# Seven-product passes that run on from chunk to chunk, and a last chunk that joins them, in a two-layer encoder

## The chip, the cores and the metric

The kernel runs on one core of a Trainium2 chip. Its engines are TensorE (PE, matrix products into PSUM; its weight loads are PEld), VectorE (DVE), ScalarE (ACT), GpSimd (POOL) and SyncE (SP, which issues most DMAs). The metric is the device time of one execution in microseconds. Each engine runs its instructions in the order in which they are written down for it; semaphores order the engines among each other.

## The reference

Two layers on an input of 256 tokens by 2048 channels, all in float32. Layer 0 mixes the tokens by pooling and attention, layer 1 by a chunkwise matrix memory; after each comes a gated MLP:

```python
def conv_ffn(x, w_up, conv_w, conv_b, w_down):
    u = x @ w_up
    up = jnp.pad(u, ((0, 0), (1, 1), (0, 0)))
    c = conv_w.astype(u.dtype)
    u = c[0] * up[:, :-2] + c[1] * up[:, 1:-1] + c[2] * up[:, 2:] + conv_b.astype(u.dtype)
    gate, val = jnp.split(u, 2, axis=-1)
    return (jax.nn.silu(gate) * val) @ w_down
...
        x = x + mixed
        x = x + conv_ffn(rms_norm(x, norm_ffn[layer]), w_up[layer], conv_w[layer], conv_b[layer], w_down[layer])
```

`w_up` is 2048 x 11264, `w_down` 5632 x 2048. The change touches only the product with `w_down`.

## The kernel before

Each float32 matrix is split into a high and a low float32r part, and a product is three matmuls: high by high, high by low, low by high. A weight block of 128 x 1024 numbers (512 KB) comes by a DMA from SP's queue into `w` (six buffers), ScalarE writes the high part into `hl` and VectorE the low part (four buffers); that is the split of a block. Everything that needs weights takes them from one stream, in the order in which PE uses them. The instructions of PE stand as the program writes them; VectorE's, ScalarE's and SP's are placed by a scheduler.

The MLP walks over 44 blocks of 128 hidden channels, in chunks of 4, 8, 8, 8, 8 and 8 blocks (chunks 0 to 5). `up` makes one block: 64 matmuls from four weight blocks (11.14 us of PE), then ScalarE and VectorE make the convolution and the gate and leave the block in `g`, high and low.

The product with `w_down` of chunk c runs in the gaps between the `up`s of chunk c + 1. Two blocks of `g` are a pair; the output has two halves of 1024 columns (half 0 and half 1), each of two blocks of 512. A direct product (`dn`) of a pair with a half is a 2 by 2 block product of eight products. The kernel instead uses the seven-product scheme of Strassen and Winograd: an A pass makes four products per pair (12 matmuls) and a B pass three (9 matmuls), with sums of `g` blocks (made by `combine`, in the plan called `mix`: four VectorE instructions and two high-low splits) and sums of weight blocks. Each product has its own PSUM bank (`pp`, four banks in the pool `ps`, A uses all four, B three), which accumulates over the pairs of one chunk. At the end of a pass `drain` adds the banks into `acc` or `x`: four instructions after A, three after B, by ScalarE the first time for some and else by VectorE. After a half's last pass `total` adds `acc` into `x` in eight VectorE instructions. Chunk 1 of layer 0 uses the scheme for half 1 only and goes direct for half 0; chunk 5 of both layers goes direct in all four blocks: `down_two` for blocks 0 and 1, `down` for blocks 2 and 3 (in layer 1 block 3 is `down_end`, the `end` matmuls). In layer 1 each block of `x` then goes to `out` by SP's queue.

The weight sums of an A pass come in two ways. For half 0 a task (`premix`) makes them long before in DRAM with DMAs (`m`), and the stream loads the result. For half 1 the stream makes them as it goes: a `Sum` is one DMA on SP's queue and a second, adding one on POOL's queue into a `sum` buffer (three buffers); a `Chain` is a load to which VectorE adds the sum (`w<-w,sum`, then `w<-w`) before it is split. So an A pass of half 1 loads three blocks per pair and costs VectorE two adds more; an A pass of half 0 loads two; a B pass one and a half.

`_ffn_plan` writes the order. Behind each `up` stands a slot with one unit: two pairs of a pass (one pair in chunk 1 of layer 0). The pass order was A, B of half 1 and then A, B of half 0, in each chunk anew. Below, A1 is an A pass of half 1, an A1 step an `up` with a unit of A1 behind it, and so on. `pp` and a chunk number in a name stand for a product of that chunk; `_14` is half 1, product 4.

Of the kernel before, what the change touches and what calls it, by code (L numbers as in the profile page):

```python
# [16 lines left out]
P = 128  # L17
# [17 lines left out]
BOTH = ((0, 2, 3, 4), (0, 1, 2, 3, 4))  # L35
NEG = -1.0e30
# [173 lines left out]
def trunk(ctx: ExitStack, tc: tile.TileContext, gx, xT, xn, call, catt, cml, weights, mixes, out):  # L210
# [749 lines left out]
    def ffn_layer(layer, norm, nxt):  # L960
        with ExitStack() as es:
# [7 lines left out]
            combos, pss, quads, seen = {}, {}, {}, set()  # L969
# [86 lines left out]
            def drain(kind, c, h, order):  # L1056
# [15 lines left out]
                if kind == "B" and c == len(FCH) - 2:  # L1072
                    wv.add(total(h), 1.5)
# [59 lines left out]
            def down_two(c):  # L1133

                gt, n = gts[c], FCH[c]
                pss2 = [mmp.tile([P, 2, 512], F32, tag="mm", name=f"dn{layer}_{c}_{b}") for b in range(2)]
                for kts in (range(n - 2), range(n - 2, n)):
                    for ps in pss2:
                        mov_part(ps, lambda k: gt[:, k], list(kts), kts[0] == 0, kts[-1] == n - 1)
                wv.until(lambda: ("A", 0) not in seen or ("total", 0) in pss)  # L1140
                for b, ps in enumerate(pss2):
# [8 lines left out]
            for kind, c, i, *j in _ffn_plan(layer):  # L1150
# [9 lines left out]
                elif kind == "two":  # L1160
                    down_two(c)
# [65 lines left out]
def _halves(layer, c):  # L1227

    return () if c in (-1, len(FCH) - 1) else (0, 1) if c in BOTH[layer] else (1,)


def _ffn_plan(layer):

    seq = []
    for c, n in enumerate(FCH):
        pairs = FCH[c - 1] // 2 if c else 0  # L1240
        halves = _halves(layer, c - 1)

        if halves == (0, 1):
            slots = [[(kind, c - 1, h, js)] for h in (1, 0) for kind in "AB"
                     for js in ((0, 1), (2, 3))[: pairs // 2]]
            slots = [[]] * (pairs < 4) + slots
        else:
            slots = [[(kind, c - 1, 1, (j,))] for kind in "AB" for j in range(pairs)]
            for b in range(2 if pairs else 0):
                slots[(b + 1) * pairs // 2 - 1].append(("down", c - 1, b))  # L1250

        busy = {j: k for k, slot in enumerate(slots) for u in slot if u[0] == "A" for j in u[3]}
        for i in range(n):
            seq.append(("up", c, i))
            seq += slots[i] if i < len(slots) else []
            if c < len(FCH) - 1:
                seq += [("mix", c, j) for j in range(n // 2) if i == max(2 * j + 1, busy.get(j, 0))]
    return seq + [("two", len(FCH) - 1, 0)] + [("down", len(FCH) - 1, b) for b in range(2, NB)]


def _down_chunks(layer, w):
# [3 lines left out]
    for c, n in enumerate(FCH):  # L1265
        rows = w[k0 * P : (k0 + n) * P]
        blocks = [_mov(rows[:, b * 512 : b * 512 + 512]) for b in range(NB) if b // 2 not in _halves(layer, c)]
# [5 lines left out]
    n = sum(FCH[:-1]) // 2  # L1273
# [12 lines left out]
def _ffn_weights(layer, up, parts):  # L1286
# [3 lines left out]
    for kind, c, i, *j in _ffn_plan(layer):  # L1290
# [3 lines left out]
        elif kind in ("down", "two"):  # L1294
            out += [next(down) for _ in range(FCH[c] // 2 * (2 if kind == "two" else 1))]
# [119 lines left out]
```

## Time and profile before

| | |
|---|---|
| time, median of 3 runs | 2163.43 us (2162.89 to 2163.73) |
| profiled execution | 2163.78 us, its span 2162.0 us |
| PE, weight loads, VectorE, ScalarE, POOL busy | 2156.2, 1844.2, 1734.7, 1414.3, 212.7 us |
| MLP of layer 0 | from 257 to 972 us of the span, the seven-product passes from 325 to 925 |
| MLP of layer 1 | from 1450 to the end, the passes from 1518 to 2115 |
| all `pp` matmuls | 1428, 361.8 us busy |
| all `dn` and `end` matmuls | 480, 111.3 us busy |
| DMA | 555.29 MB, mean 257 GB/s |

Busy time is the time in which at least one instruction of an engine ran. Instructions of PE overlap, so the mean duration of a matmul is longer than the distance between two. In the chain of waits a row is a start, a duration and a piece of work, and the chain is followed back from the last instruction; where it stays on PE, PE never waited.

### The profile page before, as it was taken

To read this page: it belongs to the slowest core of one execution; us is meant where nothing else is said; L and a number is where in the kernel's file an instruction comes from. 1 tells how busy PE (TensorE), PEld (TensorE's weight loads), DVE (VectorE), ACT (ScalarE), POOL (GpSimd) and SP (SyncE) were. 2 spreads that over 40 slices of the span, in tenths; PEclk is the share of its full clock that TensorE was granted. 3 is DMA by queue.
4 is the path that set the end of the run, shared out by engine and by line. 5 is a ranking of instruction groups with operands and counts; after the bars stand their busy time and mean duration, and the time that the engine had idled before them with its cause. 6 is when DMAs were issued, how large, how long until landed. Compare 5 with 4: busy or idle time off the path is not lost.

```text
span 2162.0 us, 31902 instructions
## 1 busy us (share of the span) xinstructions
PE 2156.2 (100%) x11412; PEld 1844.2 (85%) x11412; DVE 1734.7 (80%) x2425; ACT 1414.3 (65%) x2208; POOL 212.7 (10%) x268
## 2 busy tenths in 40 slices
PE   9999999999999999999999999999999999999999
PEld 7888888888888888889888888888888888888887
DVE  7686688887988988986777676667889898988896
ACT  7665578766777767666454544457777777776763
POOL 0022111110100100001111111211100000000000
PEclk9999999999999999999999999999999999999999
DMA  9668989898999877779888888898978787887774
GB/s 323 213 202 250 287 250 311 248 280 247 298 296 293 287 257 232 266 232 252 231 246 251 237 250 230 273 276 249 289 226 285 258 283 246 265 262 251 233 249 162
DMA packets 164097, 555.29 MB, mean 257 GB/s; under 512 B 20602, under 2 KB 23202, under 8 KB 163938
## 3 DMA queue, kind: packets, MB, share of 16 engines
q1 hardware_dynamic: 129632, 462.88, 62.0%
q0 software_dynamic: 20704, 52.71, 14.8%
q10 hardware_dynamic: 13602, 37.67, 5.7%
q8 instruction: 89, 1.46, 0.3%
q14 instruction: 70, 0.57, 0.1%
HBM read 551.04 MB, written 69.25 MB: 287 GB/s over the span
## 4 chain that ended last, share of the span: by engine, by line
PE 97%; DVE 2%; DMA 1%; issue 0%; ACT 0%; DVEq 0%
PE up L264 44%; PE pp L264 15%; PE op L264 8%; PE dn L264 5%; PE mv L264 4%; PE mq L264 4%; PE mk L264 4%; PE mo L264 4%; PE qproj L264 3%; PE kproj L264 1%; PE vproj L264 1%; PE pool L264 1%; DVE hl L128 1%; PE qk L264 1%; PE av L264 1%; PE end L264 1%
## 5 line engine op out<-in xcount | busy, mean ns | idle before, releaser
L128 DVE TENSOR_TENSOR hl<-w,hl 128x1024 fp32r<-128x1024 f32 (+2 forms) x840 | 1009.4, 1214 | 218.4 <-ACT hl L127 216.0
L127 ACT CAST hl<-w 128x1024 fp32r<-128x1024 f32 (+2 forms) x839 | 863.4, 1047 | 451.4 <-PE up L264 145.3
L264 PE MATMUL up<-xx,hl 128*128 128x512 f32 (+1 forms) x5632 | 994.0, 337 | 0.0
L264 PEld LDWEIGHTS up<-xx,hl 128*128 128x128 f32 x5632 | 866.9, 188 | 130.9 <-DVE hl L128 0.5
L264 PE MATMUL pp<-hl,s 128*128 128x512 f32 x816 | 204.9, 392 | 0.3 <-DVE hl L128 0.3
L264 PEld LDWEIGHTS pp<-hl,s 128*128 128x128 f32 x816 | 150.4, 188 | 32.0 <-DVE hl L128 1.2
L473 POOL DMA_DIRECT2D m<-m x128 | 102.1, 800 | 701.0 <-PE up L264 293.1
L264 PE MATMUL pp<-hl,g 128*128 128x512 f32 x612 | 156.9, 391 | 0.0
L427 ACT COPY tb_up<-up 128x512 f32<-128x512 f32 x88 | 51.6, 587 | 123.4 <-PE up L264 123.2
L264 PEld LDWEIGHTS pp<-hl,g 128*128 128x128 f32 x612 | 112.2, 188 | 22.3
L991 ACT ACTIVATE y<-tb_up,conv 128x256 f32<-128x256 f32 x176 | 104.4, 593 | 0.0
L992 DVE TENSOR_TENSOR y<-y,z 128x510 f32<-128x510 f32 x88 | 60.7, 689 | 52.2 <-ACT y L991 52.2
L473 POOL DMA_DIRECT2D m<-in_dn x64 | 54.6, 853 | 468.1 <-PE dn L264 168.1
L264 PE MATMUL dn<-hl,g 128*128 128x512 f32 x432 | 100.3, 391 | 0.0
L428 DVE TENSOR_TENSOR tb_up<-up,tb_up 128x512 f32<-128x512 f32 x88 | 60.8, 691 | 49.2 <-ACT tb_up L427 48.9
L264 PEld LDWEIGHTS dn<-hl,g 128*128 128x128 f32 x432 | 80.6, 188 | 16.6
L989 ACT ACTIVATE z<-tb_up,conv 128x256 f32<-128x256 f32 x176 | 88.9, 505 | 5.1 <-DVE tb_up L984 4.2
L264 PE MATMUL mk<-xx,hl 128*128 128x512 f32 (+1 forms) x512 | 92.2, 337 | 0.0
L264 PE MATMUL mq<-xx,hl 128*128 128x512 f32 (+1 forms) x512 | 92.1, 337 | 0.0
L264 PE MATMUL mv<-hl,xx 128*128 128x512 f32 (+2 forms) x480 | 91.7, 350 | 0.0
L264 PE MATMUL op<-hl,cat 128*128 128x512 f32 x384 | 91.6, 393 | 0.0
L264 PE MATMUL mo<-hl,xx 128*128 128x512 f32 x384 | 90.5, 391 | 0.0
(232 smaller groups left out, 2196.5 us busy)
## 6 DMA issues: line engine op xcount, KB each, us to landing
w<-in_up SPq DMA_DIRECT2D x352, 512.0 KB, 4.8
w<-in_dn SPq DMA_DIRECT2D x176, 512.0 KB, 4.6
w<-in_m_in SPq DMA_DIRECT2D x124, 512.0 KB, 5.1
m<-in_dn ACTq DMA_DIRECT2D x128, 256.0 KB, 5.5
w<-m SPq DMA_DIRECT2D x64, 512.0 KB, 5.0
w<-in_a_in SPq DMA_DIRECT2D x46, 512.0 KB, 5.3
sum<-in_dn SPq DMA_DIRECT2D x36, 512.0 KB, 5.4
sum<-in_dn POOLq DMA_DIRECT2D x36, 512.0 KB, 9.1
```

The source lines that it names most:

```text
L127: (self.nc.vector.tensor_copy if i + c == 0 else self.nc.scalar.copy)(hl[:, 0, c : c + n], w[:, c : c + n])
L128: low = self.nc.vector.tensor_sub(hl[:, 1, c : c + n], w[:, c : c + n], hl[:, 0, c : c + n].bitcast(F32))
L264: last_mm[0] = pe.matmul(out_, lhsT, rhs, start=start, stop=stop, skip_group_check=True)
L427: a.copy(tb, ps[:, :, 1, :])
L428: v.tensor_add(tb, ps[:, :, 0, :], tb)
L473: paced(eng.dma_start(to[p : p + P // 2], src[p : p + P // 2], **kw))
L989: a.activation(z[:, 0, j, :], u[:, j, :], AF.Copy, scale=cw(tl, 0))
L991: a.activation(y[:, j, :], u[:, j, :], AF.Identity, scale=cw(tl, 1), bias=cw(tl, 3))
L992: v.tensor_add(y[:, :, 1:S], y[:, :, 1:S], z[:, 0, :, 0 : S - 1])
```

## The change

Passes are now listed by hand, per layer and chunk. Where the last pass of a chunk and the first of the next are of the same kind and half, they are one pass: its banks are not drained between the chunks and the first product of the second does not start the bank anew. `first`, `last` and `end` of a unit are worked out from its neighbours. Layer 0 has four such joints (A1 from chunk 0 to 1, B1 from 1 to 2, B0 from 2 to 3, B1 from 3 to 4), layer 1 three (B1 from 0 to 1, B0 from 1 to 2, B1 from 2 to 3). 38 passes become 31.

In layer 1 the first two pairs of chunk 5 leave the direct path for half 1. Their A products join the A1 pass of chunk 4 and their B products its B1 pass; blocks 2 and 3 go direct with the other two pairs alone. For that, the order in chunk 5 of layer 1 is A0, A1, A1 of the new pairs, B0, B1, B1 of the new pairs. The last B1 unit of chunk 4 has no `up` behind it, and the unit of the new pairs stands between the first 36 direct matmuls of block 0 and the rest of `down_two`. total(1) follows at the very end, total(0) one `up` before the end. Two combinations more are made in chunk 5.

```diff
+LAST = (0, 4)
+PASSES = (
+    ("B0 A0 B1 A1", "A1 B1", "B1 A1 A0 B0", "B0 A1 A0 B1", "B1 A1 A0 B0"),
+    ("B0 A1 A0 B1", "B1 A1 A0 B0", "B0 A1 A0 B1", "B1 A1 A0 B0", "A0 A1 A1+ B0 B1 B1+"),
+)
...
-            def unit(kind, c, h, js):
-                n = FCH[c] // 2
+            def unit(kind, c, h, js, first, last, end):
...
-                if js[0] == 0:
+                if first:
...
-                    product(pss[e], x_, wh, wl, j == 0, j == n - 1)
-                if js[-1] == n - 1:
+                    product(pss[e], x_, wh, wl, first and j == js[0], last and j == js[-1])
+                if last:
                     pss["busy"] = True
-                    wv.add(drain(kind, c, h, order), 0.6)
+                    wv.add(drain(kind, h, order, end), 0.6)
...
-                if kind == "B" and c == len(FCH) - 2:
+                if end:
                     wv.add(total(h), 1.5)
...
-                kts = list(range(FCH[c]))
+                kts = list(range(_direct(layer, c, b), FCH[c]))
...
+            def down_two(c, second):
...
+                parts = [(ps, kts) for kts in (range(n - 2), range(n - 2, n)) for ps in twos]
+                for ps, kts in parts[1:] if second else parts[:1]:
+                    mov_part(ps, lambda k: gt[:, k], list(kts), kts[0] == 0, kts[-1] == n - 1)
+                if not second:
+                    return
...
+def _pairs(layer, c):
+    return (LAST[layer] if c == len(FCH) - 1 else FCH[c]) // 2
+def _direct(layer, c, b):
+    return LAST[layer] if c == len(FCH) - 1 and b >= NB // 2 else 0
...
+    for c in range(len(FCH) - 1):
+        at = max(at + (c == 0) * FCH[0], sum(FCH[: c + 1]))
+        step = len(_halves(layer, c))
+        for pas in PASSES[layer][c].split():
+            k = c + pas.endswith("+")
+            for j in range(0, _pairs(layer, k), step):
+                units.append((pas[0], k, int(pas[1]), tuple(range(j, j + step))))
+                to = slots[min(at, FT - 1)] if at <= FT else late
+                to.append(len(units) - 1)
...
+                at += 1
+    for n, u in enumerate(units):
+        first, last = (not 0 <= m < len(units) or (units[m][0], units[m][2]) != (u[0], u[2]) for m in (n - 1, n + 1))
+        units[n] = u[:4] + (first, last, all(o[2] != u[2] for o in units[n + 1 :]))
...
+    seq += [("two", c, 0)] + [units[e] for e in late] + [("two", c, 1)]
+    return seq + [("down", c, b) for b in range(2, NB)]
```

Three places show what moves. The first is VectorE in layer 0, at the last `up` of chunk 2 (`y_19` is its block): before, the B1 pass of chunk 1 is drained here (`pp_1_10` to `pp_1_12`), between the splits and the sum adds (`w<-w,sum`) of the A1 pass of chunk 2.

```order
L128 TENSOR_TENSOR hl_5252<-w_5174,hl_5252 128x1024
L123 TENSOR_TENSOR w_5270<-w_5270,sum_5150 128x512
L128 TENSOR_TENSOR hl_5272<-w_5199,hl_5272 128x1024
L1068 TENSOR_TENSOR acc_2469<-acc_2469,pp_1_10_4847 128x512
L1068 TENSOR_TENSOR x<-x,pp_1_11_4848 128x512
L128 TENSOR_TENSOR hl_5294<-w_5240,hl_5294 128x1024
L1068 TENSOR_TENSOR x<-x,pp_1_12_4849 128x512
L123 TENSOR_TENSOR w_5314<-w_5314,sum_5196 128x512
L124 TENSOR_TENSOR w_5270<-w_5270 128x512
L992 TENSOR_TENSOR y_19_5226<-y_19_5226,z_19_5227 128x2x255
```

Now the B1 pass of chunk 2 follows with no drain and no sum adds at this place:

```order
L134 TENSOR_TENSOR hl_5240<-w_5163,hl_5240 128x1024
L134 TENSOR_TENSOR hl_5260<-w_5185,hl_5260 128x1024
L134 TENSOR_TENSOR hl_5282<-w_5226,hl_5282 128x1024
L998 TENSOR_TENSOR y_19_5212<-y_19_5212,z_19_5213 128x2x255
L999 TENSOR_TENSOR y_19_5212<-y_19_5212,z_19_5213 128x2x255
L134 TENSOR_TENSOR hl_5303<-w_5238,hl_5303 128x1024
```

The three drain adds and the sum adds have left this place; they stand two `up`s later, together.

The second is SP in layer 1, in the second half of chunk 5: before, the loads here were premixed sums of half 0 (`m_14`, `m_15`) between those of two `up`s.

```order
L107 DMA w_19367<-in_up 128x1024
L107 DMA w_19378<-m_14_13061 128x1024
L107 DMA w_19390<-m_14_13061 128x1024
L107 DMA w_19413<-m_15_13327 128x1024
L107 DMA w_19435<-m_15_13327 128x1024
L107 DMA w_19456<-in_up 128x1024
```

Now the sums of the second and third A1 step stand there (the first three of the run are issued long before):

```order
L118 DMA sum_19183<-in_dn 128x1024
L113 DMA w_19230<-in_dn 128x1024
L118 DMA sum_19291<-in_dn 128x1024
L113 DMA w_19270<-in_dn 128x1024
L113 DMA w_19294<-in_up 128x1024
L113 DMA w_19345<-in_up 128x1024
L113 DMA w_19359<-in_up 128x1024
L113 DMA w_19372<-in_up 128x1024
L118 DMA sum_19356<-in_dn 128x1024
L113 DMA w_19393<-in_dn 128x1024
```

Four loads of finished sums became three sums in the ring of three buffers, and the loads to which they are added.

The third is PE at the end of layer 1, behind the last `up`. Before, the last B0 products of chunk 4 are followed by direct products alone (block 0, block 1, then the last pair of each):

```order
L264 MATMUL pp_4_02_19809<-hl_19948,s_4_3_18793 128x512 x3
L264 MATMUL dn_5_0_19979<-hl_19959,g_5_18798 128x512 x12
L264 MATMUL dn_5_0_19979<-hl_19970,g_5_18798 128x512 x12
L264 MATMUL dn_5_0_19979<-hl_19983,g_5_18798 128x512 x12
L264 MATMUL dn_5_1_19980<-hl_20001,g_5_18798 128x512 x12
```

Now the B1 pass stays open over the first 36 matmuls of block 0 and takes the new pairs of chunk 5 in (`g_5`, `s_5`):

```order
L270 MATMUL pp_4_12_19932<-hl_19971,s_4_3_18745 128x512 x3
L270 MATMUL dn_5_0_20005<-hl_19983,g_5_18750 128x512 x12
L270 MATMUL dn_5_0_20005<-hl_19995,g_5_18750 128x512 x12
L270 MATMUL dn_5_0_20005<-hl_20009,g_5_18750 128x512 x12
L270 MATMUL pp_4_10_19930<-hl_20026,g_5_18750 128x512 x3
L270 MATMUL pp_4_11_19931<-hl_20026,g_5_18750 128x512 x3
L270 MATMUL pp_4_10_19930<-hl_20043,g_5_18750 128x512 x3
L270 MATMUL pp_4_11_19931<-hl_20043,g_5_18750 128x512 x3
L270 MATMUL pp_4_12_19932<-hl_20060,s_5_0_19224 128x512 x3
L270 MATMUL pp_4_12_19932<-hl_20060,s_5_1_19340 128x512 x3
L270 MATMUL dn_5_1_20006<-hl_20071,g_5_18750 128x512 x12
```

Eighteen matmuls of the B1 pass came in; blocks 2 and 3 have two rows of twelve instead of four each. Over the whole program PE has 24 matmuls of A and 18 of B more and 48 direct ones fewer; VectorE 22 drain adds fewer; SP three loads and POOL two adding DMAs more.

More of the change, by code (lines that the diff above doesn't have):

```diff
@@ L1227, in _halves @@
 def _halves(layer, c):
[L1229 to L1252 removed]
+    return () if c == len(FCH) - 1 else (0, 1) if c in BOTH[layer] else (1,)
@@ L1253, in _ffn_plan @@
         for i in range(n):
             seq.append(("up", c, i))
[L1255 to L1258, printed above, removed]
+            mixes = [(busy.get((c - 1, j), 0) - f0, ("mix", c, j)) for j in range(_pairs(layer, c))]
+            mixes = [(k, e) for k, e in mixes if i == max(2 * e[2] + 1, k)]
@@ L1266, in _down_chunks @@
         rows = w[k0 * P : (k0 + n) * P]
-        blocks = [_mov(rows[:, b * 512 : b * 512 + 512]) for b in range(NB) if b // 2 not in _halves(layer, c)]
+        blocks = [_mov(rows[_direct(layer, c, b) * P :, b * 512 : b * 512 + 512]) for b in range(NB) if b // 2 not in _halves(layer, c)]
         if c == len(FCH) - 1:
@@ L1294, in _ffn_weights @@
         elif kind in ("down", "two"):
-            out += [next(down) for _ in range(FCH[c] // 2 * (2 if kind == "two" else 1))]
+            n = FCH[c] // 2 - 1
+            out += [next(down) for _ in range((n, n + 2)[i] if kind == "two" else (FCH[c] - _direct(layer, c, i)) // 2)]
         elif kind != "mix":
```

27 lines of the change are left out of this document (17 added, 10 removed).

## Prediction

> **What bounds the kernel now.** I read the page first, for who is busy and which engine the chain of waits runs through, then that chain in order of time, to get prices and to see where it leaves TensorE.
>
> ```profile
> span 2162.0 us, 31902 instructions
> ...
> PE 2156.2 (100%) x11412; PEld 1844.2 (85%) x11412; DVE 1734.7 (80%) x2425; ACT 1414.3 (65%) x2208; POOL 212.7 (10%) x268
> ...
> PE 97%; DVE 2%; DMA 1%; issue 0%; ACT 0%; DVEq 0%
> ```
>
> The chain lies on PE for 97% of the span and PE idles 2162.0 - 2156.2 = 5.8 us in all. So a change gains only by taking matmuls away or by ending what little waiting there is, and loses by making new waiting. Five rows of the chain give the prices of matmuls; one shows where it leaves PE:
>
> ```profile
> 477.96 10.88 PE dn L264 x48
> ...
> 555.94 8.55 DMA w<-in_dn
> ...
> 586.66 4.10 PE pp L264 x18
> ...
> 617.14 5.53 PE pp L264 x24
> 2114.72 32.64 PE dn L264 x144
> 2147.36 10.89 PE end L264 x48
> 2158.28 0.69 DVE x L1114
> ```
>
> A direct matmul takes 10.88/48 = 0.2267 us, one of an A pass 5.53/24 = 0.2304, one of a B pass 4.10/18 = 0.2278, each at its full pace. The second row is the exception: at 556 us the chain runs through a weight load of layer 0. To see what such places cost, busy time by stretch, each cut at the start of an `up`: two A steps of half 1 (first, fourth, fifth and sixth row), and what follows the first of them.
>
> ```profile
> core 0: us, PE busy (x) PEld busy (x) DVE busy (x) ACT busy (x) POOL busy (x), PEclk, DMA share, GB/s
> 541.45:575.36 33.91, 33.61 (x178) 28.39 (x176) 31.86 (x44) 24.86 (x37) 3.81 (x5) 1.00 0.95 293
> 575.36:605.84 30.48, 30.48 (x165) 26.21 (x164) 27.09 (x37) 22.29 (x35) 4.36 (x6) 1.00 1.00 310
> 605.84:639.17 33.33, 33.33 (x177) 28.47 (x176) 28.88 (x38) 24.92 (x41) 1.56 (x2) 1.00 0.88 297
> 669.65:703.27 33.62, 33.61 (x177) 28.39 (x176) 31.13 (x43) 24.31 (x37) 3.30 (x5) 1.00 0.93 292
> 1859.31:1892.63 33.32, 33.32 (x177) 28.47 (x176) 32.42 (x45) 24.18 (x37) 2.85 (x4) 1.00 0.86 275
> 1986.93:2020.26 33.33, 33.33 (x177) 28.47 (x176) 32.43 (x45) 24.18 (x37) 0.85 (x1) 1.00 0.68 219
> ```
>
> Two A steps take 33.33 us where nothing is late. In layer 0 they take 33.91 and 33.62: 0.58 and 0.29 us of waiting, 0.87 together, the only stalls that I find in either MLP. VectorE's waits in those two stretches have one row each:
>
> ```profile
> DVE w L123 <- DMA w<-in_dn: 2.0, 1, 2.0
> DVE w L123 <- DMA w<-in_dn: 2.4, 1, 2.4
> ```
>
> The in-order VectorE waits for a load (the one that it adds the sum to), and the splits queued behind that add reach PE late. Of 2.0 and 2.4 us of waiting PE feels 0.58 and 0.29: a lead of some 1.4 to 2.1 us absorbs the rest. In layer 1 VectorE is as busy (32.43 of 33.33 us) and PE loses nothing. The granted clock is 1.00 everywhere, so it is no part of this.
>
> **The change part by part.** *Matmuls.* Two pairs of chunk 5 leave the direct path in half 1 of layer 1: 24 `dn` and 24 `end` matmuls go, 24 A and 18 B ones come. That is 24 x 0.2304 + 18 x 0.2278 - 24 x 0.2267 - 24 x 10.89/48 = 5.53 + 4.10 - 5.44 - 5.45 = -1.26 us, all on PE and so all on the path.
>
> *Drains.* Seven joints disappear (six B, one A), 6 x 3 + 4 = 22 adds of VectorE; the 16 first copies of ScalarE stay. The new pairs add VectorE and ScalarE work. Prices, from groups of instructions in layer 0's MLP:
>
> ```profile
> L128 DVE TENSOR_TENSOR hl<-w,hl 128x1024 fp32r<-128x1024 f32 x225 | 270.9, 1220 | 23.8 <-ACT hl L127 23.5
> L1068 DVE TENSOR_TENSOR acc<-acc,pp 128x512 f32<-128x512 f32 x23 | 15.2, 680 | 0.0
> L123 DVE TENSOR_TENSOR w<-w,sum 128x512 f32<-128x512 f32 x18 | 12.4, 687 | 7.0 <-DMA w<-in_dn 7.0
> L1013 DVE TENSOR_TENSOR s<-sf,s 128x384 fp32r<-128x384 f32 x17 | 9.4, 552 | 0.0
> L1006 DVE TENSOR_TENSOR sf<-s 128x256 f32<-128x256 f32 x17 | 7.1, 420 | 0.1
> L1007 DVE TENSOR_TENSOR sf<-sf,s 128x128 f32<-128x128 f32 x17 | 4.9, 286 | 0.1
> ```
>
> Removed: 22 x 0.680 = 15.0 us. Added: three more splits (3.66), four sum adds (4 x 0.687 = 2.75) and two combinations, each 0.552 + 0.420 + 3 x 0.286 = 1.83 (3.66), together 10.1 us. VectorE's total falls by 4.9 us; that is worth nothing as long as PE is the chain. The drains were hidden under the next `up` (11.1 us on PE against 4 x 0.68) and the splits stay ahead of PE. The 10.1 us all fall into chunk 5 of layer 1, where the number of drains does not change (14 before and now).
>
> *The A steps of half 1.* A pass that goes on into the next chunk forces the order B, A, A, B where it was A, B, A, B. In layer 0, A1 steps now follow two B1 steps and are followed by two A0 steps, in chunks 2 and 3. An A1 step loads 10 blocks of 0.524 MB, an A0 step 8, a B step 7. The first two stretch rows moved 33.91 x 293 + 30.48 x 310 = 19.4 MB against 34 blocks = 17.8 MB, so the premixing adds 1.6 MB, 0.8 per pair of steps. At the 310 GB/s of the row with the DMA share 1.00, two A1 steps need (10.5 + 0.8)/0.310 = 36.4 us and have 33.3: 3.1 us short, whatever stands around them. Two A0 steps need 29.7 of 33.3 and give 3.6 back. So the shortage ends where it ended, and I keep the 0.87 us of layer 0's stalls: change 0, bounds -0.87 (the A1 steps come 30 us later, when less premixing is left) and +1.7 (each of three chunks like the worst one).
>
> *Three A1 steps in a row.* In layer 1 the last chunk now has A1 steps at its third, fourth and fifth `up`. By the last stretch row VectorE has 1.5 x 32.43 = 48.6 us of work in 50.0: it fits, with 1.4 us to spare. Each step issues two more sums, one DMA on SP's queue and behind it one on POOL's, in a ring of three buffers, so sum n waits for the split of sum n - 3. Rows of sums, from the last stretch and, for the loads, from the last two:
>
> ```profile
> L123 DVE TENSOR_TENSOR w<-w,sum x4: 683/684/686, 1987.3 to 2009.1; 128x512 f32<-128x512 f32 x4
> L112 SPq DMA_DIRECT2D sum<-in_dn x1: 327/327/327, 1995.7 to 1995.7; - x1
> L113 POOL DMA_DIRECT2D sum<-in_dn x1: 850/850/850, 1999.8 to 1999.8; - x1
> ...
> sum<-in_dn SPq DMA_DIRECT2D x1, 512.0 KB, 3.5
> sum<-in_dn POOLq DMA_DIRECT2D x1, 512.0 KB, 5.5
> ...
> sum<-in_dn SPq DMA_DIRECT2D x4, 512.0 KB, 4.3
> sum<-in_dn POOLq DMA_DIRECT2D x3, 512.0 KB, 8.5
> ...
> DMA to landing us min/median/max: 3.5/8.0/17.7
> ```
>
> The fourth sum is issued at 1995.7 and used at 2009.1, 13.4 us later. It needs 4.1 us to POOL's issue and 5.5 to land: 3.8 us in hand at a DMA share of 0.68. With the landings of the busier stretch (4.3 and 8.5, and 0.6 between) it needs 13.4: nothing in hand. The new sixth sum stands to the third as the fourth to the first; the fifth has longer. So two sums sit at the edge. Bounds: 0 (they land as at 1995) and 2 x 0.58 = 1.2 us (each costs what the worst wait of layer 0 cost). I take 0.3, nearer the rows of layer 1, whose A1 steps at shares of 0.86 and 0.68 lose nothing.
>
> A rule of the Trainium skill speaks against this step. SBUF — State Buffer, section "SBUF: two separate sides", says that DMAs from GpSimd's queue have their descriptors made on GpSimd, whose SBUF ports VectorE can hold for a whole instruction, and counts a VectorE instruction with two SBUF inputs among those that can block one reading SBUF. By it each new POOL sum could land one split later, an estimate of 1.2 us, and with the two edge sums at their upper bound the whole sum would be an estimate of +0.2 us; the POOL row above (850 ns for the issue beside a VectorE 97% busy) shows no such stretch.
>
> *Queues.* SP takes three loads more and POOL two, 5 x 0.524 = 2.6 MB, all in the last 100 us, where they replace nothing but time in which SP waited for free buffers. All output DMAs still stand behind the last load on SP.
>
> *The tail.* The late B1 unit ends with 36 + 12 + 12 + 24 + 24 = 108 matmuls, 24.5 us, still to run. In that time VectorE drains it (3 adds), makes total(1) (8), adds four residuals of blocks 0 and 1, two of block 2, and six splits: 17 x 0.68 + 6 x 1.22 = 18.9 us. Block 2's PSUM tile is block 0's, whose residuals are added while block 1 still takes 2.7 us. What counts is the end: while block 2 runs (5.4 us) VectorE has two residuals, a split and five adds of total(1), 2 x 0.68 + 1.22 + 5 x 0.68 = 6.0 us, 0.5 too much; then three more adds (2.0) before the first `end` add, due 9.5 us after block 2 began. 8.0 of 9.5: 1.5 us in hand. Block 2's output (512 KB, landing in 3.0 us)
>
> ```profile
> out<-x SPq DMA_DIRECT2D x3, 512.0 KB, 3.0
> ```
>
> now starts 3.5 us before PE ends instead of 10, and is out of the way of the last two. Cost 0, bounds 0 and 0.7.
>
> *Sum.* -1.26 + 0 + 0.3 + 0 = -0.96 us. The profiled execution took 2163.78 us, 1.8 around its span and 0.35 above the median of 2163.43; it would take 2162.8, the median 2162.5. With the bounds: -1.26 - 0.87 = -2.1 to -1.26 + 1.7 + 1.2 + 0.7 = +2.3, so 2161.3 to 2165.8.
>
> **Rivals.** *Late sums (slower).* If POOL's sums land late in the three A1 steps, VectorE waits with every split behind it. It has 1.4 us to spare and a lead of about 1.5, then each us goes to PE. At the longest landing that any sum shows, 17.7 us, a sum is 4.1 + 17.7 - 13.4 = 8.4 us late; two of them cost 16.8 - 2.9 = 13.9, and the time is 2163.4 - 1.3 + 13.9 = 2176. Slower by over 0.2% needs 4.3 + 1.3 = 5.6 us on PE, 8.5 of waiting, so two landings over 13.6 us. For it: 48.6 of 50.0 us, and loads of 315 GB/s in such a step (5.24 MB in 16.67 us). Against it: no premixing runs then, and three pairs of A1 steps in layer 1 stand without loss.
>
> *The DMA ceiling in layer 0 (slower).* A1, A1, A0, A0 need 36.4 + 29.7 = 66.1 us of DMA in 66.7. If the buffers are not full when such a run begins, the 3.1 us of shortage show whole, in three chunks: 9.3 - 0.9 - 1.3 = +7.1, 2170.5; half of that stays at 2166. Against it: two B steps before the run need 13.2 us each of 15.25 and refill the buffers.
>
> *VectorE sets the time (faster).* In the A1 steps VectorE is 97% busy and PE's weight loads 28.47 of 33.33 us, 85%. If VectorE, and not PE, paced the MLPs, the time would follow its 4.9 us: 2163.4 - 4.9 = 2158.5. Against it: PE keeps its 33.33 us at any VectorE load in the rows, and the chain is on VectorE for 2%. The Trainium skill, Perfetto Trace Analysis, section "Identifying the Most-Contended Engine", reads it that way: matmul busy time is a poor measure, the weight loads' share and VectorE's occupancy are good ones. The chain decides against it here.
>
> **How the numbers follow.** A measurement of this kernel can tell about 0.2%, 4.3 us, from no change. The forecast (2161.3 to 2164) has 0.76; late sums or the ceiling in part, up to 2167.7, have 0.10; late sums in full 0.08, the ceiling in full 0.04; VectorE as the pace 0.02. So faster 0.02, same 0.86, slower 0.12. The range 2160.9 to 2166.6 leaves out the 0.12 above, the 0.02 below and some 0.03 of the partial cases.
>
> **What would show it.** Right: 11,406 PE instructions; the A1 pairs of layer 1 still 33.33 us; the three A1 steps 50.0 us with VectorE waiting under 2 us for DMA; stalls in layer 0 of about 0.9 us at the A1 steps, 30 us later than now; the last `end` row followed by one VectorE add. Wrong: a chain that leaves PE in the three A1 steps or for long in A1, A1, A0, A0 of layer 0, total(1) on the chain at the end, or a pace of `pp` other than 0.228 to 0.230 us. The forecast fails if waiting of more than 5 us appears anywhere.

## The result, and the profile after

| | before | after |
|---|---|---|
| median | 2163.58 us (2162.89 to 2164.24, 10 runs) | 2169.18 us (2166.51 to 2171.57, 10 runs) |
| ratio | | 1.0024, 95% interval 1.0016 to 1.0033 |
| profiled execution, span | 2163.78, 2162.0 us | 2171.57, 2169.5 us |

The change costs 5.6 us where a gain of 0.96 was forecast. The profiled execution after is the slowest of its ten, so single terms read from it come out somewhat larger than in the median. One execution of the kernel before, among those beside e5 to e8 below, took 6063.23 us and is left out of the medians.

I read the page first, as before: the engines' busy time and the shares of the chain.

```profile
span 2169.5 us, 31918 instructions
...
PE 2159.2 (100%) x11406; PEld 1846.2 (85%) x11406; DVE 1730.9 (80%) x2420; ACT 1415.8 (65%) x2215; POOL 214.3 (10%) x270
...
PE 95%; DVE 3%; DMA 2%; issue 1%; ACT 0%; DVEq 0%; POOLq 0%; ACTq 0%
```

PE runs the forecast number of instructions, 11,406, but its busy time has grown by 3.0 us where 1.26 were to go, and its idle time from 5.8 to 10.3 us. So there is waiting, and there are also matmuls that run slower. The timeline of PE at the third A1 step of chunk 5 in layer 1, the step of the new pairs, has both (start, duration, work; in brackets the idle time before it and what ended it):

```profile
2066.52 2.24 PE L270 MATMUL pp<-hl,s 128*128 128x512 f32 x9
2068.60 0.86 PE L270 MATMUL pp<-hl,g 128*128 128x512 f32 x3
2069.67 0.72 PE L270 MATMUL pp<-hl,s 128*128 128x512 f32 x2 [0.21 <-ACT s L1018]
2073.19 3.35 PE L270 MATMUL pp<-hl,s 128*128 128x512 f32 x7 [2.79 <-DVE s L1019]
2076.34 1.48 PE L270 MATMUL pp<-hl,g 128*128 128x512 f32 x3
2077.62 11.98 PE L270 MATMUL up<-xx,hl 128*128 128x512 f32 x64
```

The step's 24 matmuls take 2077.62 - 2066.52 = 11.10 us instead of 5.53. The first twelve, those of the first new pair, run at full pace. The first product of the second pair starts two of its three matmuls and then waits 2.79 us for `s` from VectorE's line 1019, which writes the low part of that pair's combination. Behind the gap seven matmuls take 3.15 us from the first start to the start of what follows, twice the usual 1.6. The chain of waits says why the combination was late. It leaves PE at 2020.11, 53 us earlier, and runs over ScalarE and VectorE until it comes to these rows:

```profile
2037.44 7.79 DMA w<-in_dn
...
2045.32 0.69 DVE w L129
...
2046.82 1.15 DVE hl L134
2047.97 0.02 issue
2047.98 5.99 DMA sum<-in_dn
...
2054.53 8.52 DMA sum<-in_dn
2063.06 0.02 issue
2063.08 0.69 DVE w L129
...
2072.66 0.48 DVE s L1019
2073.14 0.04 issue
2073.19 4.63 PE pp L270 x10
```

The sixth sum may only be issued at 2047.98, when the split of the third has freed the ring's buffer. That split stood on VectorE behind an add that had waited for a load. The first DMA lands after 5.99 us, POOL's after 8.52 more, and only then, at 2063.08, can VectorE add the sum. Behind that add stand, in VectorE's order, five splits, the last steps of the hidden block from which the combination is made, and the combination, until 2073.14. VectorE's waits between 2021 and 2078 us (engine, line and releaser: us in total, times, longest):

```profile
DVE w L129 <- DMA sum<-in_dn: 1.7, 1, 1.7
DVE w L129 <- DMA w<-in_dn: 0.9, 1, 0.9
```

Only 2.6 us of waiting for DMAs, and PE loses more than that. Busy time by stretch: the first two A1 steps, the third, the end of the gap, what follows the gap (the first half of that third step lies before both), and for comparison the two A1 steps of layer 0 with the stall there:

```profile
core 0: us, PE busy (x) PEld busy (x) DVE busy (x) ACT busy (x) POOL busy (x), PEclk, DMA share, GB/s
2021.66:2055.38 33.72, 33.67 (x177) 28.31 (x176) 32.79 (x45) 23.51 (x34) 2.55 (x3) 1.00 0.81 264
2055.38:2077.62 22.24, 19.24 (x90) 15.56 (x89) 19.88 (x29) 15.30 (x25) 0.00 (x1) 0.88 0.72 219
...
2072.25:2073.19 0.94, 0.00 (x1) 0.01 (x1) 0.94 (x3) 0.94 (x3) 0.00 (x0) 0.50 0.91 336
2073.19:2079.05 5.86, 5.86 (x15) 4.70 (x16) 5.20 (x8) 3.47 (x6) 0.00 (x0) 0.50 0.76 215
...
588.86:623.00 34.14, 33.60 (x177) 28.39 (x176) 29.33 (x38) 22.55 (x35) 4.97 (x6) 1.00 1.04 330
```

For 5.86 us behind the gap the granted clock is 0.50. So the third step and the `up` behind it (11.81 us to the next `pp` instead of 11.14) cost 5.57 + 0.67 = 6.2 us: 0.21 + 2.79 = 3.0 of idle time, some 2.9 by the clock (half of 5.86), and the rest at the edges of the gaps, which the brackets leave out. Where a loss of PE without a bracket is given below, it is counted so, from start to start, beyond the usual spacing. In layer 0 the two A1 steps take 34.14 us, 0.81 more than 33.33. The first two A1 steps of chunk 5 take 33.72, 0.39 more.

One place more was not forecast. In layer 1's first chunk, where nothing waited before, the chain now has

```profile
1558.63 1.23 DVE hl L134
1559.86 0.04 issue
1559.90 6.31 PE up L270 x35
```

and PE starts these matmuls 0.98 us late. The end of the program is as forecast, the last product followed by one add; only the two B1 units behind the last `up` take 8.57 us (2119.93 to 2128.50) in place of 8.20:

```profile
2159.96 5.45 PE end L270 x24
2165.42 0.02 issue
2165.44 0.69 DVE x L1121
```

These terms, 6.2 + 0.4 + 1.0 + 0.4 less the 1.26 of matmuls, make 6.7 of the 7.5 us between the two spans; the rest is spread over places of under 0.3 us each.

Not every execution paid for the clock. Of the ten after, the four with a mean granted clock of 1.000 took 2166.51 to 2168.78 us, the four with 0.999 took 2169.14 to 2170.04 and the two with 0.998 took 2170.33 and 2171.57. All ten of the kernel before are under 2164.3.

### The profile page after: what moved, and what is told of

Read it like the earlier page. It is cut to its first block, busy times and chain, and to the rows that moved or that the text cites. A ratio compares the mean times of both kernels' runs of the same rounds, so it can differ in the third digit from the quotient of the medians.

```text
span 2169.5 us, 31918 instructions
## 1 busy us (share of the span) xinstructions
PE 2159.2 (100%) x11406; PEld 1846.2 (85%) x11406; DVE 1730.9 (80%) x2420; ACT 1415.8 (65%) x2215; POOL 214.3 (10%) x270
## 4 chain that ended last, share of the span: by engine, by line
PE 95%; DVE 3%; DMA 2%; issue 1%; ACT 0%; DVEq 0%; POOLq 0%; ACTq 0%
PE up L270 43%; PE pp L270 14%; PE op L270 8%; PE dn L270 4%; PE mv L270 4%; PE mq L270 4%; PE mk L270 4%; PE mo L270 4%; PE qproj L270 3%; DVE hl L134 1%; PE kproj L270 1%; PE vproj L270 1%; PE pool L270 1%; DMA sum<-in_dn 1%; DMA w<-m 1%
## 5 line engine op out<-in xcount | busy, mean ns | idle before, releaser
L270 PE MATMUL pp<-hl,s 128*128 128x512 f32 x840 | 213.1, 395 | 3.7 <-DVE s L1019 2.8
L270 PEld LDWEIGHTS pp<-hl,s 128*128 128x128 f32 x840 | 155.5, 189 | 37.7 <-DVE s L1019 3.2
L270 PE MATMUL pp<-hl,g 128*128 128x512 f32 x630 | 162.1, 392 | 0.0
L270 PE MATMUL dn<-hl,g 128*128 128x512 f32 x408 | 95.0, 391 | 0.0
L270 PE MATMUL op<-hl,mcat 128*128 128x512 f32 x384 | 89.5, 392 | 0.0
```

The costliest lines, as they stand in the source:

```text
L270: last_mm[0] = pe.matmul(out_, lhsT, rhs, start=start, stop=stop, skip_group_check=True)
```

## The experiments

Theory 1 is what the chain after shows: the sums that the stream makes as it goes, in three A1 steps in a row, come too late, and the late one holds up the combination that stands behind it on VectorE. The rivals stand in the expectations. Ratios are to the kernel before, measured beside each run on the same chip. The ratio on record is not exactly the quotient of the two medians (for e1 that would be 1.0006), and the interval belongs to the ratio.

| run | median us | before us | ratio, 95% interval |
|---|---|---|---|
| e1_joints_only | 2164.79 | 2163.43 | 1.0008 (0.9999 to 1.0017) |
| e2_last_only | 2169.00 | 2163.43 | 1.0025 (1.0015 to 1.0034) |
| e3_no_sixth_sum | 2165.27 | 2163.43 | 1.0010 (1.0001 to 1.0019) |
| e4_later_join | 2168.59 | 2163.43 | 1.0022 (1.0013 to 1.0032) |
| e5_old_combination | 2164.72 | 2163.80 | 1.0006 (0.9997 to 1.0015) |
| e6_half0_last | 2167.70 | 2163.80 | 1.0016 (1.0007 to 1.0025) |
| e7_half0_joints | 2170.31 | 2163.80 | 1.0030 (1.0019 to 1.0042) |
| e8_joints_layer0 | 2163.52 | 2163.80 | 1.0001 (0.9991 to 1.0010) |
| e9_premixed_last | 2164.55 | 2163.76 | 1.0004 (0.9995 to 1.0013) |
| e10_half0_later | 2165.68 | 2163.76 | 1.0007 (0.9998 to 1.0016) |
| e12_premix_pace | 2164.53 | 2163.40 | 1.0002 (0.9993 to 1.0011) |
| e13_joints_late | 2163.88 | 2163.40 | 1.0001 (0.9992 to 1.0010) |

### The two parts apart: joints alone, new pairs alone

The first run keeps the joints and leaves the last chunk direct; the second keeps the pass order of before and joins only the two new pairs.

```diff
 # e1_joints_only
-LAST = (0, 4)
+LAST = (0, 0)
...
-    ("B0 A1 A0 B1", "B1 A1 A0 B0", "B0 A1 A0 B1", "B1 A1 A0 B0", "A0 A1 A1+ B0 B1 B1+"),
+    ("B0 A1 A0 B1", "B1 A1 A0 B0", "B0 A1 A0 B1", "B1 A1 A0 B0", "A0 A1 B0 B1"),
 # e2_last_only
-    ("B0 A0 B1 A1", "A1 B1", "B1 A1 A0 B0", "B0 A1 A0 B1", "B1 A1 A0 B0"),
-    ("B0 A1 A0 B1", "B1 A1 A0 B0", "B0 A1 A0 B1", "B1 A1 A0 B0", "A0 A1 A1+ B0 B1 B1+"),
+    ("A1 B1 A0 B0", "A1 B1", "A1 B1 A0 B0", "A1 B1 A0 B0", "A1 B1 A0 B0"),
+    ("A1 B1 A0 B0", "A1 B1 A0 B0", "A1 B1 A0 B0", "A1 B1 A0 B0", "A0 A1 A1+ B0 B1 B1+"),
```

> The seven joints alone: chunk 5 of layer 1 goes direct as before, the order of passes and the longer passes are those of the change. Theory 1 (PE waits in the third A1 step for the combination of the second new pair, which stands on VectorE behind the late sixth sum): no such step here, so the 6.2 us go; 1.3 us of matmuls come back; about 2164 us, with stalls of 1 to 2 us in layer 0 as in the changed kernel. Rival (the joints and their pass order cost the time, by A1 steps that meet A0 steps): 2167 us or more.

> The two new pairs of chunk 5 alone: passes in the old order and drained in every chunk, but for the last chunk of layer 1, whose order is that of the change. Theory 1: the stall of the third A1 step stays, 3 to 6 us with the slower clock behind it, so 2166 to 2170 us. Rival (the joints cost the time): 2162 to 2163 us.

Joints alone: +1.4 us, with an interval that reaches just below none. New pairs alone: +5.6 us, the whole loss. The timeline of PE in the second run has the gap at the same product, with none of the joints there:

```profile
2068.16 0.74 PE L270 MATMUL pp<-hl,s 128*128 128x512 f32 x2 [0.28 <-ACT s L1018]
2071.76 2.64 PE L270 MATMUL pp<-hl,s 128*128 128x512 f32 x7 [2.86 <-DVE s L1019]
2074.20 1.49 PE L270 MATMUL pp<-hl,g 128*128 128x512 f32 x3
```

and its chain has the same sixth sum, issued at 2046.73, its DMAs 5.99 and 8.35 us. The two parts apart add up to more than they cost together (6.9 against 5.6); the intervals are too wide to make something of that.

### The sixth sum taken away

```diff
-                if i:
+                if i and c == len(FCH) - 1 and q - q0 == 1:
+                    out += [s0[q], r[q]]
+                elif i:
```

> The changed kernel, in which the second new pair's A products take plain weight blocks: its sum (one DMA on SP's queue, one on POOL's) and the two adds of VectorE are left out, and so are two matrix sums of the computation. Theory 1, where the late sum is the first cause: VectorE's wait of 1.7 us at the sum goes, the combination is ready 2 to 4 us earlier, PE's gap of 2.8 us and the slow clock behind it go, about 2163 us. Rival (the combination is late by itself, because its block is made only one step ahead): a gap of 1 to 2 us stays, and with it the slow clock, 2166 to 2168 us.

The second new pair's A weights are plain loads here, so the kernel leaves out the sixth sum, its two DMAs and two adds of VectorE (1.2 to 1.4 us of work); the joints stay, as in e4 and e5 below. +1.8 us in place of +5.6, between the two forecasts: the sixth sum carries about 3.8 us, its part of the slow clock included. At the product of the second new pair is left

```profile
2069.54 1.89 PE L270 MATMUL pp<-hl,s 128*128 128x512 f32 x7 [0.50 <-DVE s L1019]
```

0.50 us of waiting for the same combination, and its matmuls at the usual pace. So the sixth sum is most of it, by its lateness and its adds together; a small rest is the combination's own.

### The combination taken off the way

Does PE wait because splits of weights are late, or only because the combination is?

```diff
-                s3 = kp.tile([P, 2, 3, P], F32R, tag=f"s3{j}", name=f"s3{layer}_{c}_{j}")
+                s3 = combos[c - 1, j][0] if c == len(FCH) - 1 else kp.tile([P, 2, 3, P], F32R, tag=f"s3{j}", name=f"s3{layer}_{c}_{j}")
...
-                for d, e in ((s3, sf[:, 0:3]), (s1, sf[:, 3])):
+                for d, e in ((s3, sf[:, 0:3]), (s1, sf[:, 3]))[c == len(FCH) - 1 :]:
```

> The A products of the two new pairs use chunk 4's sums of g blocks: the part of the two combinations in chunk 5 that A products need (two VectorE and two ScalarE instructions, 1.1 us of VectorE) is left out; sums of weights and all matmuls stay. Theory 1 (PE waits for the second combination, which stands on VectorE behind the wait for the sixth sum; the clock falls because of that long gap): no gap over 1 us in the third A1 step, no doubled spacing of matmuls, VectorE still waits 1 to 2 us for the sixth sum, time 2164 to 2166. Theory 2 (the late splits of the sixth sum's block are enough by themselves, the combination is only the last of several late things): a gap of 1.5 us or more remains, at a weight tile instead of at s, and the time stays at 2167 to 2169.5.

The A products of the two new pairs take chunk 4's sums here, and the part of the combination that they need is left out. +0.9 us, as theory 1 forecast, and less than the joints alone cost. VectorE's waits between 2020 and 2075 us are even longer than after, 3.9 us in place of 2.6:

```profile
DVE w L129 <- DMA w<-in_dn: 2.7, 1, 2.7
DVE w L129 <- DMA sum<-in_dn: 1.2, 1, 1.2
```

and yet PE runs the third A1 step without a gap, 2073.05 - 2067.53 = 5.52 us:

```profile
2067.53 2.24 PE L270 MATMUL pp<-hl,s 128*128 128x512 f32 x9
2069.60 0.85 PE L270 MATMUL pp<-hl,g 128*128 128x512 f32 x3
2070.30 2.22 PE L270 MATMUL pp<-hl,s 128*128 128x512 f32 x9
2072.36 0.86 PE L270 MATMUL pp<-hl,g 128*128 128x512 f32 x3
```

It loses 0.58 and 0.35 us at the longer of the two waits, in the step before; with the edges, that step and the `up` behind it take 17.87 us (2049.66 to 2067.53) in place of 16.67, 1.2 more. So late weights cost little: their splits run ahead of PE. What is made only one step ahead of its use, and behind the late add, is the combination. That separates the two theories, although the edit also takes 1.1 us of work off VectorE.

### The join one step later

```diff
-    ("B0 A1 A0 B1", "B1 A1 A0 B0", "B0 A1 A0 B1", "B1 A1 A0 B0", "A0 A1 A1+ B0 B1 B1+"),
+    ("B0 A1 A0 B1", "B1 A1 A0 B0", "B0 A1 A0 B1", "B1 A1 A0 B0", "B0 A0 A1 A1+ B1 B1+"),
```

> The changed kernel with chunk 5 of layer 1 in the order B0, A0, A1, A1 of the new pairs, B1, B1 of the new pairs. The three A1 steps are the fifth to seventh; both combinations are made from blocks that are two and three steps old, and B0 joins the pass before it. Theory 1: no wait for a combination even if sums land late; 2162.0 to 2163.5 us, or 1.0 to 1.5 us more if the sums themselves hold the splits. Rival (three A1 steps in a row are too much for VectorE and the loads): the gap stays at the third A1 step, 2166 us or more.

+5.2 us: the forecast of theory 1 missed, and the time is that of the rival. No DMA is late here, but VectorE has no time left. Busy time over the two A0 steps (first row) and the two A1 steps of chunk 4 that follow them (second):

```profile
2018.53:2051.86 33.33, 33.33 (x178) 28.47 (x177) 27.51 (x36) 24.02 (x38) 0.00 (x0) 1.00 0.75 246
2051.86:2088.78 36.92, 34.41 (x178) 28.08 (x176) 36.89 (x51) 23.45 (x32) 2.56 (x3) 1.00 0.82 244
```

VectorE is busy 36.89 of 36.92 us: the drain of A0 and the eight adds of total(0) now fall into the steps with the sums, and both combinations are made there too. PE waits up to

```profile
2087.51 0.74 PE L270 MATMUL pp<-hl,s 128*128 128x512 f32 x2 [1.70 <-DVE hl L134]
```

and the next matmuls keep their pace. The two steps take 3.6 us more than 33.33, the larger part of the loss; the joints' stalls, which this run keeps (0.92 us at 1559.62 among them), and 0.69 us of waiting at 2124.49 are in it too. So theory 1 lacks a half: these steps have no slack on VectorE, and in this run the work placed there showed on PE, late sum or not.

### The same pairs with premixed sums

```diff
 # e9_premixed_last: e2_last_only with
-                if i:
+                if i and c < len(FCH) - 1:
 # e12_premix_pace: e9_premixed_last with
-                        premix(1, 30.0, 30.0, 0)
+                        premix(1, 27.0, 27.0, 0)
```

> As the run with the two new pairs alone (no joints), but their two weight sums for half 1 are premixed in DRAM like those of half 0, and the A steps of the new pairs load the results: no sum in the ring and four VectorE adds fewer in the third A1 step; both combinations stay in full. Theory 1 (sums made on the fly are the cause): no wait of VectorE for a load in chunk 5 of over 0.5 us, no gap of PE over 0.7 us there, and the matmuls' 1.26 us come out: 2162.0 to 2163.2. Theory 4 (the combination is late by VectorE's load alone, whoever makes the sums): a gap of 1 us or more before the second pair's A products remains, 2164.5 to 2168.

> As the run with premixed sums for the two new pairs, but the premixing of layer 1, which has 20 pairs in place of 18, goes at a pace of 27 instead of 30 us per pair, so that it ends when it ended before. If the two small stalls of that run's profile (0.5 us in layer 0, 0.6 us at 1555 us) came from premixing that runs on into the first chunk: the one at 1555 is gone and the time is 2162.3 to 2163.6. If the denser premixing takes bandwidth from layer 0's end or the matrix memory: new stalls between 900 and 1500 us, 2164 or more.

Both combinations are complete here; only the sums of the new pairs are made elsewhere. The three A1 steps, first two and third:

```profile
2020.91:2054.63 33.72, 33.70 (x177) 28.31 (x176) 33.45 (x46) 23.51 (x33) 0.85 (x1) 1.00 0.71 222
2054.63:2071.30 16.67, 16.67 (x90) 14.23 (x89) 13.96 (x20) 13.06 (x24) 0.00 (x0) 1.00 0.74 245
```

50.39 us against 55.43 in e2, which is the same but for the sums, and 55.96 after: the loss there is gone but for 0.39. VectorE has 33.45 + 13.96 = 47.4 us of work in them. With the four adds of the two sums it would be 49.8 to 50.2 in 50.0 (0.60 each from start to start in a packed row, 0.687 by duration): that is the slack that the change had, none.

Neither time is the gain that was hoped for. In e9 the gap is gone as theory 1 says, but 2164.55 lies in theory 4's range. Its profile has stalls of 0.5 and 0.6 us elsewhere, at 574 and at 1555 us. In e12, with premixing at the faster pace, neither is there. For the one at 574 that can't be the pace: layer 1's premixing begins in layer 0's last chunk, and the profiles of e2 and e10, at the old pace, lack it too. The time of e12, 2164.53, is that of its second forecast, but the new stalls between 900 and 1500 us that should go with it are not in its profile.

The span of e12's profile, 2161.0 us, is 1.0 below that of before. That is not the 1.26 us of matmuls by itself: this execution lacks the 0.87 us of layer 0's stalls, and has 0.39 of new loss in the first A1 step and 0.4 in the last B1 units. It is also the second fastest of its eleven. Their median is 2164.53 (2162.61 to 2167.22) beside 2163.40 (2162.65 to 2166.65) of before: no difference that can be told, so a gain of the kernel is not shown. What the slower executions lose is open; the two above 2167 have a mean granted clock of 0.999.

### The new pairs in half 0

```diff
 # e6_half0_last: half 0, pass order of before, no joints
-    return LAST[layer] if c == len(FCH) - 1 and b >= NB // 2 else 0
+    return LAST[layer] if c == len(FCH) - 1 and b < NB // 2 else 0
...
+    ("A1 B1 A0 B0", "A1 B1 A0 B0", "A1 B1 A0 B0", "A1 B1 A0 B0", "A1 A0 A0+ B0 B0+ B1"),
 # e7_half0_joints: the same with the joints of the changed kernel
 # e10_half0_later: e6_half0_last with
-    seq += [("two", c, 0)] + [units[e] for e in late] + [("two", c, 1)]
+    seq += [("two", c, 0), ("two", c, 1)] + [units[e] for e in late]
```

> The passes of before, with no joint between chunks, and in layer 1 the two pairs of chunk 5 join the last A and B pass of half 0 instead of half 1, whose weight sums are premixed in DRAM: no sums in the ring, no adds of VectorE. Theory 1 (the loss of the changed kernel comes from the sums made on the fly in three steps in a row): the 1.26 us of matmuls come out, 2162.0 to 2163.0 with under 0.5 us of new stalls in chunk 5 of layer 1. Theory 3 (two more pairs overload VectorE or PE's order at the end wherever they are put): 2165 or more.

> As the run with half 0, with the joints between chunks of the changed kernel kept. Theory 1: the joints add the 0.7 to 1.4 us that they cost alone, 2163.0 to 2164.5. If joints help when VectorE is less loaded (22 drain adds less): below the run without them, under 2162.

> As the run with half 0 and no joints, but the last B1 unit is put behind all direct products of blocks 0 and 1 instead of behind the first twelve. If the 1.5 us that PE waits there for the residual of block 0 comes from the B1 drain that stands ahead of it on VectorE: that wait goes to under 0.3 us and the time falls by 1 to 2 us, to 2165.5 to 2166.7. If VectorE is short of time in the whole tail (25.7 of 26.4 us busy there): the wait moves to total(1) at the end, and the time stays at 2167 to 2168.5.

Half 0 has its sums premixed, and in the A steps of chunk 5 nothing is late. But the end pays: in the first run PE stands still behind the last B1 unit, in the last 50 us,

```profile
2139.77 11.16 PE L270 MATMUL dn<-hl,g 128*128 128x512 f32 x48 [1.30 <-DVE x L443]
```

for the residual of block 0, whose PSUM tile block 2 takes. The B1 drain and adds of total(0) stand ahead of that residual, and only 36 direct matmuls of blocks 0 and 1 are left to cover them. This execution also lost 1.4 us at the A1 steps of layer 0, which the edit does not touch. Theory 3 of the expectation (the end is overloaded) is right for this order. With the unit behind all of blocks 0 and 1 that wait is gone from the profile, as forecast, and the loss is 1.9 us in place of 3.9, though the two intervals overlap. With the joints the run is the slowest of all, +6.5 us, far above both of its forecasts. Its profile has the same 1.30 us at 2140.45, 0.69 at 623 and 1.08 at 1560; but at 2168.47 it is the fastest of the six executions, and does not show what the others lose. Why that one is so slow stays open.

### Where the joints cost

> Joints of layer 0 alone; layer 1 as before. If the joints' cost (2164.8 against 2163.5 in the run with all of them and no new pairs) lies in both layers alike: 2163.8 to 2164.4, with stalls at 621 us near 0.9 to 1.5 us and none at 1560. If layer 1 carries it: 2163.2 to 2163.6; if layer 0 carries all: 2164.5 to 2165.

```diff
 # e8_joints_layer0 and e13_joints_late
-LAST = (0, 4)
+LAST = (0, 0)
 # e8_joints_layer0: layer 1 as before
-    ("B0 A1 A0 B1", "B1 A1 A0 B0", "B0 A1 A0 B1", "B1 A1 A0 B0", "A0 A1 A1+ B0 B1 B1+"),
+    ("A1 B1 A0 B0", "A1 B1 A0 B0", "A1 B1 A0 B0", "A1 B1 A0 B0", "A1 B1 A0 B0"),
 # e13_joints_late: joints of layer 1 from its second chunk on
+    ("A1 B1 A0 B0", "B0 A1 A0 B1", "B1 A1 A0 B0", "B0 A1 A0 B1", "B1 A1 A0 B0"),
```

> Joints alone, as in the first run, but layer 1 begins with the old order A1 B1 A0 B0 in its first chunk, and its four joints (B0, B1, B0, B1) start from the second. If the cost of the joints is the order A1, A0 in the first chunk while premixing still fills the DMA: no stall near 1560 us, 2163.2 to 2164.0. If joints in layer 1 cost wherever they stand: 2164.4 to 2165.2.

Joints in layer 0 alone show no cost (-0.3 us, interval over both signs): one stall of 1.03 us at 621.68, behind a premixed load that took 13.73 us, has taken the place of the two of before. With joints in layer 1 from its second chunk on the time is 2163.88 beside 2163.40, and no stall stands near 1560. Busy time of that stretch, with all joints and then with the late ones:

```profile
1518.00:1580.00 62.00, 61.42 (x327) 52.30 (x326) 54.72 (x72) 48.30 (x76) 10.23 (x13) 1.00 0.95 289
1518.00:1580.00 62.00, 62.00 (x331) 53.08 (x330) 53.68 (x70) 48.83 (x78) 10.00 (x13) 1.00 0.97 292
```

In the run with all joints the chain of waits had there

```profile
1541.19 12.16 DMA w<-in_up
...
1560.14 5.96 PE up L270 x33
```

a load that took 12.16 us. All six kernels with the order A1, A0 in layer 1's first chunk (after, e1, e3, e4, e5, e7) start PE 0.2 to 1.1 us late between 1559 and 1561. Of the eight others only e9 and e10, which premix more sums, have a stall near there (0.6 us at 1555 and 0.5 at 1539). So the cost of the joints that a profile shows, about 1 us, goes with that order and not with the joints as such. That premixing, which still runs there, makes the loads late is argued and not shown: the DMA share is 0.95 with the stall and 0.97 without it. The medians differ by less than their intervals here; it is the place of the stalls that decides.

## Why the prediction was wrong

*Matmuls*: right. The count is as forecast, and the units take their 4.10 (B) and 5.53 us (A) and the direct matmuls their 0.227 where nothing is late. No run shows the 1.26 us as a shorter time of the kernel.

*Drains*: right in what mattered. VectorE's total fell by 3.8 us (4.9 forecast), and no time with it. The price was somewhat high: with the joints alone VectorE's busy time went from 1734.7 to 1722.0, 12.7 us for 22 adds, 0.58 each and not 0.68, since VectorE instructions that follow each other overlap: in the trace after two of 0.68 us each start 0.60 apart, at 2031.25 and 2031.85.

*The A steps of half 1*: right for layer 0, 0.81 us at the two A1 steps now, 0.87 in all before, and nothing that can be told for joints there alone. That the numbers are so close is luck: with layer 0 as before, both places take 33.33 us in the profiles of e10 and e12, and 33.70 and 34.33 in that of e6. The upper bound of 1.7 was a slip too: three chunks at 0.58 are 1.7 in all, so 0.87 more than before. The step looked at layer 0 only. The same shortage appeared in layer 1's first chunk, where the order A1, A0 was also new and premixing was also still running: about 1 us.

*Three A1 steps in a row* is the step that failed. It gave 0.3 us with an upper bound of 1.2; it cost 6.2 in the profiled execution, and the new pairs alone, with no joint, cost the whole 5.6 us of the median. Three things were wrong in it.

First, the spare time. 1.5 times the stretch of two A1 steps in layer 1 gave 48.6 us of VectorE work; by the run with premixed sums and the price of four adds it is 49.8 to 50.2 of 50.0. The combinations of chunk 5 and the drains of the passes before fall into these steps together, and the stretch that I scaled had another mix.

Second, the landing. The 13.4 us from issue to use were right: VectorE reached its add at 2063.08 - 1.70 = 2061.38, 13.4 us after the sum's issue. The need, put at 13.4 too, was not. The sum took 15.1: 5.99 us for the first DMA, 0.56 to POOL's issue and 8.52 for the second. The median of the busier stretch, 4.3 us, was taken for the first DMA. So it was late by 1.7 us.

Third, and this is the size: the price of a late sum. I took 0.58 us, what PE had felt of a wait of 2.0 in layer 0. That price holds for weights, whose splits run ahead of PE; the run with the old combination shows it again, 3.9 us of waiting on VectorE for 1.2 on PE. But in the third step the second pair's combination stands behind the late add, and it is made one step before its use, since the second block of that pair comes from the `up` of the step before. The last VectorE steps of that block (the product with the gate, its low part) stand behind the late add as well. No lead is there to absorb anything. PE stood still for 2.79 us, and the clock behind the gap cost some 2.9 more. The prediction had the clock at 1.00 everywhere and gave a stall no second price. The queue behind the waiting instruction held not only splits, and the prediction named only these.

*Queues*: right. POOL's issues of the sums took their usual time, next to a VectorE that was busy for 32.79 of 33.72 us (min, median, max ns):

```profile
L119 POOL DMA_DIRECT2D sum<-in_dn x3: 850/850/857, 2035.3 to 2054.5; - x3
```

so the rule of the Trainium skill that was weighed there (SBUF — State Buffer, "SBUF: two separate sides") did not decide; the second DMA landed as in the busier stretch (8.5 us) and it was the first, on SP's queue, that took longer. The sum given beside that rule has a slip: with 1.2 in place of 0.3 it is -0.06, not +0.2.

*The tail*: within its bounds, 0.4 at the B1 units and nothing at the end.

The rival *Late sums* named the mechanism and asked far too much of it: 8.5 us of VectorE waiting for a loss of 5.6 on PE, by landings over 13.6 us. 2.6 us of waiting did it, with no landing over 8.9. With the true price its chance would have been the larger one. *The DMA ceiling* did not come in layer 0, where the two A1 steps moved 330 GB/s and not the 310 taken as the most; the stall of 0.98 us in layer 1 is a seventh of its price, and *VectorE sets the time* was wrong as a gain, though VectorE did set the pace in these steps: work added there showed (e4), the 22 adds taken away elsewhere did not.

## What to carry to other kernels

When a step is to be lengthened, list what stands in each in-order queue behind every instruction that may wait, and give each of these its own lead over its consumer: waits of 3.9 us cost 1.2 through weights that were split ahead, and waits of 2.6 cost 6.2 through an operand made one step before its use. The work of the engine in a new sequence of steps is counted instruction by instruction, not scaled from a stretch with another mix. And where a buffer ring ties a load to work of three loads ago, the margin is to be taken with the longest landings of that stretch, not with the medians.

## What the runs showed of the hardware

PE's clock fell at gaps of 2.79 us (after) and 2.86 us (new pairs alone). In the first it was still 1.00 at 2072.20 and then 0.50 until 2079.05, 6.8 us in all; it fell 1.8 us after PE had stopped, while PE still stood. In the second PE ran 0.9 us at full pace behind the gap; then the clock was 0.50 for 3.4 us, and the spacing of the matmuls doubled. After gaps of 1.70 and 1.30 us the next matmuls kept their pace. So the stall cost 6.2 us for 3.0 of idle time in the one and 5.3 for 3.1 in the other, up to twice its length.

A gap at the same place need not bring the clock down: of the ten executions after, four kept a mean granted clock of 1.000, and of the nine with the new pairs alone two did; these are the fastest of their kernels. In e1, e3, e4 and e5, whose profiles have no gap over 1.70 us, no execution is under 1.000.

The Trainium skill, TensorE: Matmul & The Clock Gate, section "What's actually happening", has this gate: half rate after an idle window of about 3.4 us, full rate again after as long a busy one. The trace agrees in the rate, and in the recovery once (3.4 us of busy PE) and once not (5.9 us); and a gap of 2.8 us was already enough in both profiled executions that had one.
